# A hybrid four-mixer transformer block: element-wise steps change engine, and weight splits come in pieces

## The chip, the core and the metric

The kernel runs on one core of a Trainium2 chip. That core has TensorE (PE in the profile; its weight loads stand apart as PEld), VectorE (DVE), ScalarE (ACT), GpSimd (POOL), SyncE (SP, which issues most of the DMAs) and 16 DMA engines. The metric is the device time of one execution, in microseconds; lower is better.

## The reference, cut to what matters

One layer over 2048 tokens of width 1024. A projection feeds four mixers of width 256 each; a second projection and a SwiGLU feed-forward of width 2816 follow, with RMS norms around both.

```python
a = rms_norm(h, ln_mix_pre)
(s5_u, hg_q, hg_f, ..., fox_q, fox_k, fox_v, fox_f, ml_q, ml_k, ml_v, ...) = split(a @ w_in)
y_a = s5_mixer(...)      # complex recurrence, 16 groups
y_b = hgrn2_mixer(...)   # gated linear attention: scores(t,s) = sum_k q k exp(b_t - b_s), b = cumsum(log f)
y_c = fox_mixer(...)     # softmax(q k^T / 8 + F_t - F_s) v over all earlier tokens, head-wise RMS norm, gain
y_d = mlstm_mixer(...)   # chunked linear attention with exponential gates
h = h + rms_norm(concat[y_a, y_b, y_c, y_d] @ w_out, ln_mix_post)
a = rms_norm(h, ln_ffn_pre)
h = h + rms_norm((silu(a @ w_gate) * (a @ w_up)) @ w_down, ln_ffn_post)
```

All of it is float32. The kernel reaches that on TensorE by splitting each operand into a rounded part `hi` (type fp32r) and a rest `lo`, and adding the products hi·hi, hi·lo and lo·hi.

## The kernel before, in words

The sequence is cut into four blocks of 512 tokens. The input projection runs in two halves of two blocks each. After its first half come the mixers of block 0, in its second half the hgrn mixer of block 1 and the output projection of block 0. Then, for b = 0 to 3: output projection of b (`attn.proj`), mixers of b+1 (`mlstm_mix`, `fox_mix`, `hgrn_mix` of b+2, once `s5_mix`), feed-forward of b (`ffn`). The mixers of b+1 are written ahead of the feed-forward of b, and the two are interleaved on the engines: the program is built with `schedule_with_timeline_sim=True`, so a planner that simulates the program with its own costs sets each engine's instruction order. Every engine then runs its own queue strictly in order, and waits on semaphores.

The steps that matter here:

- `split_load` (lines 71 to 95) brings a weight tile `wr` (or `dr`) of up to 1056 columns from HBM, rounds it on ScalarE to `wh` (`dh`, line 87), and GpSimd forms the rest `wl` (`dl`, line 88) as one instruction over the whole width. Both parts are then stored for the later blocks. So weights are split only in the first pass; later passes load the stored parts.
- `fox_mix`, inner function `attend`: for each head and each tile of 128 keys, TensorE forms scores (lines 886 to 889), ScalarE takes the exponential twice, once as float32 (`f_pe`, 894) and once rounded (`f_ph`, 895), VectorE forms the rest `f_pl` (896), GpSimd adds `f_pe` to the running softmax denominators `f_accs` (900; for the first key tile it copies, 898), and TensorE multiplies with the values (903). `f_pe` lies in a ring of two buffers. The key tiles on the diagonal are narrower than 512 columns.
- `fox_mix`, inner function `output`: the normed head is multiplied with its gain on GpSimd (864).
- `hgrn_mix`: for each of two head pairs and each of the six spans h = 64 to 2 of a recursive halving, GpSimd forms the difference `hd` of the cumulative log gate and its value at the span's middle (500), ScalarE exponentiates it (504, 505), VectorE multiplies it into `hK` (507) and `hQ` (511), TensorE forms scores (521), and VectorE writes them under a mask into `hA` (525). One more difference per pair is on line 529. So a block has 14 such differences.
- `mlstm_mix`: the queries of two heads are copied into the two halves of a zero-padded tile `mQ` on GpSimd (690), four instructions in a block.

GpSimd also computes the reciprocal roots of all norms (lines 67 and 68) and sets small tiles to constants, among them the row `m01` and the tile `R` of `mlstm_mix` (lines 647, 648, 657).

Of the kernel before, what the change touches and what calls it, by code (L numbers as in the profile page):

```python
# [8 lines left out]
F32 = mybir.dt.float32  # L9
# [3 lines left out]
AF = mybir.ActivationFunctionType  # L13
ALU = mybir.AluOpType
# [4 lines left out]
P = 128  # L19
# [13 lines left out]
def f32(ap):  # L33
    return ap.bitcast(F32)
# [36 lines left out]
def split_load(c, pool, raw, tag, width, shape, src, key=None, part=None):  # L71

    nc = c.nc
    n = shape[0] * shape[1]
    hi = pool.tile([P, width], F32R, name=tag + "h", tag=tag + "h")[:, 0:n]
    lo = pool.tile([P, width], F32R, name=tag + "l", tag=tag + "l")[:, 0:n]
    if key in c.parts:  # L80
        a = part or 0
        for t, d in zip((hi, lo), c.parts[key]):
            nc.sync.dma_start(f32(t), d[:, a:a + n])
    else:
        r = raw.tile([P, width], F32, name=tag + "r", tag=tag + "r")[:, 0:n]
        nc.sync.dma_start(r.rearrange("p (k n) -> p k n", k=shape[0]), src)
        nc.scalar.activation(hi, r, AF.Copy)  # L87
        nc.gpsimd.tensor_tensor(lo, r, f32(hi), ALU.subtract)  # L88
        if key is not None:
            c.parts[key] = kept = [c.dram.tile([P, n], F32, name=f"{key}{x}") for x in "hl"]  # L90
            for t, d in zip((hi, lo), kept):
                nc.sync.dma_start(d, f32(t))
    return [x.rearrange("p (k n) -> p k n", k=shape[0]) for x in (hi, lo)]
# [76 lines left out]
def l3(t):  # L170
    return t.rearrange("p (c l) -> p c l", l=P)
# [277 lines left out]
def hgrn_mix(c, b):  # L449
    nc, tc = c.nc, c.tc  # L450
    with ExitStack() as ctx:
# [3 lines left out]
        p1, p2, ptmp = tp("h_p1", 1), tp("h_p2", 2), tp("h_tmp", 4)  # L455
# [32 lines left out]
        for p in range(2):  # L488
            A4 = hA[p].rearrange("p h (c l) -> p h c l", l=P)
            for i, h in enumerate(LEVELS):  # L490
                w = 2 * h
                nb = BLK // w
                q3 = qs[p].rearrange("p (n w) -> p n w", w=w)
                k3 = ks[p].rearrange("p (n w) -> p n w", w=w)
                Q = hQ[(7 * p + i) % nk]
                if h > 1:
                    b3 = bs[p].rearrange("p (n w) -> p n w", w=w)
                    dd = tmp("hd")
                    d3 = dd.rearrange("p (n w) -> p n w", w=w)
                    nc.gpsimd.tensor_tensor(d3, b3, b3[:, :, h - 1:h].to_broadcast([P, nb, w]), ALU.subtract)  # L500
                    ee = tmp("he")
                    eq = ee[:, 0:256].rearrange("p (n w) -> p n w", w=h)
                    ek = ee[:, 256:512].rearrange("p (n w) -> p n w", w=h)
                    nc.scalar.activation(ek, d3[:, :, 0:h], AF.Exp, scale=-1.0)
                    nc.scalar.activation(eq, d3[:, :, h - 1:2 * h - 1], AF.Exp)
                    K = hK[(7 * p + i) % nk]
                    nc.vector.tensor_tensor(K.rearrange("p (n w) -> p n w", w=w)[:, :, 0:h],
                                            k3[:, :, 0:h], ek, ALU.mult)
                    for hh in range(2):
                        s = slice(64 * hh, 64 * hh + 64)  # L510
                        nc.vector.tensor_tensor(Q[s, hh].rearrange("p (n w) -> p n w", w=h),  # L511
                                                q3[s, :, h - 1:2 * h - 1], eq[s], ALU.mult)
                else:
                    K = ks[p]
                    for hh in range(2):
                        s = slice(64 * hh, 64 * hh + 64)
                        nc.gpsimd.tensor_copy(Q[s, hh].rearrange("p (n w) -> p n w", w=1), q3[s, :, 0:1])
                pt = ps()
                p3 = pt.rearrange("p (h t) -> p h t", h=2)
                for t in range(4):  # L520
                    nc.tensor.matmul(p3[:, :, t * 64:(t + 1) * 64], lhsT=K[:, t * P:(t + 1) * P],  # L521
                                     rhs=Q[:, :, t * 64:(t + 1) * 64], start=True, stop=True)
                av = hA[p].rearrange("p h (n w) -> p h n w", w=w)[:, :, :, h - 1:2 * h - 1]
                mv = c.lvl[:, i].rearrange("p (n w) -> p n w", w=h)[:, None].to_broadcast([P, 2, nb, h])
                nc.vector.copy_predicated(av, mv, pt.rearrange("p (h n w) -> p h n w", h=2, w=h))  # L525
            q, k, bb = qs[p], ks[p], bs[p]
            b3 = l3(bb)
            e1, e2 = tmp("he1"), tmp("he2")
            nc.gpsimd.tensor_tensor(l3(e2), b3, b3[:, :, P - 1:P].to_broadcast([P, 4, P]), ALU.subtract)
            nc.scalar.activation(e1, bb, AF.Exp)  # L530
            nc.scalar.activation(e2, e2, AF.Exp, scale=-1.0)
            nc.vector.tensor_tensor(q, e1, q, ALU.mult)
            nc.vector.tensor_tensor(k, e2, k, ALU.mult)
            qes.append(q)
            kds.append(k)
            pt = ps()
            pl = pt[:, 0:8].rearrange("p (h t) -> p h t", h=2)
            for t in range(4):
                nc.tensor.matmul(pl[:, :, t], lhsT=kds[p][:, t * P:(t + 1) * P], rhs=hL[p][:, :, t],
                                 start=True, stop=True)  # L540
            nc.vector.tensor_copy(A4[:, :, :, P - 1], pl)
# [58 lines left out]
def mlstm_mix(c, b):  # L600
    nc, tc = c.nc, c.tc
    with ExitStack() as ctx:
# [82 lines left out]
        for h in range(4):  # L685
            p = h // 2
            if h % 2 == 0:
                for hh in range(2):
                    s = slice(64 * hh, 64 * hh + 64)
                    nc.gpsimd.tensor_scalar(mQ[s, hh], qs[p][s], 1.0, None, ALU.mult)  # L690
            pw_ = ps()
            nc.tensor.matmul(pw_, lhsT=c.selr[:, h], rhs=ngh, start=True, stop=False)
            nc.tensor.matmul(pw_, lhsT=c.selr[:, h], rhs=ngl, start=False, stop=False)
# [71 lines left out]
def fox_mix(c, b):  # L765
    nc, tc = c.nc, c.tc
    NK = 4 * (b + 1)
    with ExitStack() as ctx:
# [74 lines left out]
        def output(h, po, accs):  # L843
# [17 lines left out]
            nc.vector.tensor_reduce(ms, sq, AX.X, ALU.add)  # L861
            rsqrt_mean(c, ms, ms, 64)
            nc.vector.tensor_tensor(o, o, ms[:, :, None].to_broadcast([P, 4, 64]), ALU.mult)
            nc.gpsimd.tensor_tensor(o, o, gain[:, None, h * 64:h * 64 + 64].to_broadcast([P, 4, 64]), ALU.mult)
            col = 512 + h * 64
            nc.sync.dma_start(c.y_d[b][:, col:col + 64].rearrange("(t p) n -> p t n", p=P), o)

        def attend(h):
# [6 lines left out]
            for j in range(b + 1):  # L875
# [3 lines left out]
                for i in range(4):  # L879
# [8 lines left out]
                    if diag:  # L888
                        nc.tensor.matmul(pt[:, j0 * P:j0 * P + P], lhsT=c.identb, rhs=c.mask_kq,
                                         start=False, stop=True)  # L890
                    pe = p2.tile([P, 512], F32, name="f_pe", tag="pe")
                    ph = pp.tile([P, 512], F32R, name="f_ph", tag="f_p")
                    pl = pp.tile([P, 512], F32R, name="f_pl", tag="f_p")
                    nc.scalar.activation(pe[:, cs], pt[:, cs], AF.Exp)  # L894
                    nc.scalar.activation(ph[:, cs], pt[:, cs], AF.Exp)  # L895
                    nc.vector.tensor_tensor(pl[:, cs], pe[:, cs], f32(ph[:, cs]), ALU.subtract)  # L896
                    if kt == 0:
                        nc.gpsimd.tensor_copy(accs, pe)
                    else:
                        nc.gpsimd.tensor_tensor(accs[:, cs], accs[:, cs], pe[:, cs], ALU.add)  # L900
                    terms = ((V[:, i], ph, po[:, cs]), (V[:, i, 0:64], pl, po[0:64, cs]))
                    for n, (w, r, o) in enumerate(terms if kt < NK - 1 else terms[::-1]):
                        nc.tensor.matmul(o, lhsT=w, rhs=r[:, cs], start=(kt + n == 0), stop=(kt + n == NK))  # L903
# [798 lines left out]
```

## Time and profile before

| | us |
|---|---|
| median of 3 runs | 2805.01 (2796.91 to 2816.34) |
| the profiled execution's own time | 2805.62 |
| its span, first to last instruction | 2803.9 |

The profiled execution lies within 0.1% of the median, and its own time is 1.7 us more than its span. In the rows below, PE, DVE, ACT and POOL are TensorE, VectorE, ScalarE and GpSimd, and L88 is line 88 of the kernel. An instruction's duration includes the time in which it has started and is held up inside the engine.

### The profile page before, as it was taken

How to read it: one execution, taken by the hardware profiler on the slowest of the kernel's cores; microseconds unless marked ns; L12 is line 12 of the kernel's file. 1: busy time of each engine (PE TensorE's matmuls, PEld its weight loads, DVE VectorE, ACT ScalarE, POOL GpSimd, SP SyncE). 2: the span in 40 equal slices, each digit the busy share in tenths (PEclk: the TensorE clock that was granted, in tenths of full speed). 3: DMA queues.
4: the chain of work that ended last, by engine and by line, in shares of the span. 5: the costliest groups of instructions: out<-in, count | busy, mean ns of one | idle time of the engine just before them, and what ended most of it. 6: DMA issues, size and time to landing. Idle time of an engine off the chain costs nothing.

```text
span 2803.9 us, 39055 instructions
## 1 busy us (share of the span) xinstructions
PE 2692.5 (96%) x14294; PEld 2270.0 (81%) x14294; DVE 1541.4 (55%) x2522; ACT 778.3 (28%) x1502; POOL 837.9 (30%) x927
## 2 busy tenths in 40 slices
PE   6898999999999999999899999999999999999998
PEld 5787987988888778787787788888878788888886
DVE  7958466483225665865466656545666554322333
ACT  5322336233223333324221232222122331200001
POOL 7554311243125567542111234211022330100001
PEclk9899999999999999999999999999999999999999
DMA  6573696535778878696756566575656656755553
GB/s 228 195 261 123 207 293 209 169 122 210 241 230 292 287 258 282 201 310 232 255 172 214 198 195 206 177 285 187 215 181 194 202 182 230 285 195 186 193 195 135
DMA packets 323103, 605.04 MB, mean 216 GB/s; under 512 B 56160, under 2 KB 146144, under 8 KB 322656
## 3 DMA queue, kind: packets, MB, share of 16 engines
q1 hardware_dynamic: 321888, 602.48, 64.2%
q8 instruction: 113, 1.85, 0.3%
q14 instruction: 78, 0.64, 0.1%
q0 software_dynamic: 1024, 0.07, 0.0%
HBM read 428.42 MB, written 173.35 MB: 215 GB/s over the span
## 4 chain that ended last, share of the span: by engine, by line
PE 73%; DVE 9%; DMA 8%; issue 3%; POOL 2%; SPq 2%; ACT 2%; POOLq 0%; DVEq 0%; ACTq 0%
PE pf L1469 29%; PE pf L1494 15%; PE pf L1386 6%; PE pf L288 5%; PE pf L270 5%; PE ps L903 2%; DVE hQ L511 2%; PE ps L887 1%; PE ps L886 1%; PE ps L828 1%; DVE hA L525 1%; DMA b_xt<-in_x_dram 1%; PE pt L102 1%; PE ps L521 1%; DMA wh<-wu1h 1%
## 5 line engine op out<-in xcount | busy, mean ns | idle before, releaser
L1469 PE MATMUL pf<-b_ah,wh 128*128 128x512 f32 (+1 forms) x1536 | 580.5, 378 | 4.4 <-ACT b_ah L104 4.4
L1469 PE MATMUL pf<-b_ah,wl 128*128 128x512 f32 (+1 forms) x1536 | 579.8, 378 | 0.0
L1469 PE MATMUL pf<-b_al,wh 128*128 128x512 f32 (+1 forms) x1536 | 578.2, 378 | 0.0
L1494 PE MATMUL pf<-dh,g_h 128*128 128x512 f32 x1408 | 461.3, 396 | 1.8 <-DVE b_acc L1499 1.5
L1469 PEld LDWEIGHTS pf<-b_ah,wh 128*128 128x128 f32 x1536 | 291.3, 190 | 60.4 <-ACT b_ah L104 5.3
L1469 PEld LDWEIGHTS pf<-b_ah,wl 128*128 128x128 f32 x1536 | 291.3, 190 | 55.0
L1469 PEld LDWEIGHTS pf<-b_al,wh 128*128 128x128 f32 x1536 | 289.5, 189 | 54.4
L1494 PEld LDWEIGHTS pf<-dh,g_h 128*128 128x128 f32 x1408 | 264.8, 189 | 58.7 <-DVE b_acc L1499 3.4
L1494 PE MATMUL pf<-dl,g_h 128*128 128x512 f32 x704 | 277.5, 394 | 0.0
L1499 DVE TENSOR_TENSOR b_acc<-b_acc,pf 128x512 f32<-128x512 f32 x320 | 215.7, 684 | 105.9 <-PE pf L1494 103.5
L900 POOL TENSOR_TENSOR f_accs<-f_accs,f_pe 128x512 f32<-128x512 f32 (+3 forms) x144 | 172.7, 1199 | 293.6 <-ACT f_pe L894 290.7
L88 POOL TENSOR_TENSOR wl<-wr,wh 128x1024 fp32r<-128x1024 f32 (+2 forms) x76 | 185.6, 2444 | 208.6 <-ACT wh L87 137.3
L896 DVE TENSOR_TENSOR f_pl<-f_pe,f_ph 128x512 fp32r<-128x512 f32 (+3 forms) x160 | 184.6, 1162 | 88.9 <-ACT f_ph L895 75.7
L288 PE MATMUL pf<-wl,aTh 128*128 128x256 f32 (+2 forms) x768 | 220.7, 287 | 0.2 <-DMA wl<-wi_1l 0.2
L288 PE MATMUL pf<-wh,aTh 128*128 128x256 f32 (+2 forms) x768 | 220.7, 288 | 0.0
L288 PE MATMUL pf<-wh,aTl 128*128 128x256 f32 (+2 forms) x768 | 220.2, 287 | 0.0
L1473 ACT ACTIVATE g_th<-pf 128x512 f32<-128x512 f32 x88 | 52.5, 597 | 412.2 <-PE pf L1469 412.1
L1474 DVE SCALAR_TENSOR_TENSOR g_th<-g_th,pf 128x512 f32<-128x512 f32 x88 | 60.3, 685 | 191.8 <-ACT g_th L1473 191.5
L270 PE MATMUL pf<-aTh,wh 128*128 128x512 f32 (+1 forms) x400 | 158.9, 398 | 2.7 <-ACT aTh L104 2.7
L270 PE MATMUL pf<-aTh,wl 128*128 128x512 f32 (+1 forms) x400 | 157.7, 395 | 0.0
L270 PE MATMUL pf<-aTl,wh 128*128 128x512 f32 (+1 forms) x400 | 156.9, 394 | 0.1
L1475 DVE TENSOR_TENSOR g_th<-g_th,pf 128x512 f32<-128x512 f32 x88 | 60.2, 684 | 174.8 <-PE pf L1469 174.7
(510 smaller groups left out, 4812.7 us busy)
## 6 DMA issues: line engine op xcount, KB each, us to landing
dh<-wd_0h SPq DMA_DIRECT2D x66, 256.0 KB
dl<-wd_0l SPq DMA_DIRECT2D x66, 256.0 KB
dh<-wd_1h SPq DMA_DIRECT2D x66, 256.0 KB
dl<-wd_1l SPq DMA_DIRECT2D x66, 256.0 KB
wr<-in_w_ffn_gate_dram SPq DMA_DIRECT2D x22, 512.0 KB
wr<-in_w_ffn_up_dram SPq DMA_DIRECT2D x22, 512.0 KB
dr<-in_w_ffn_down_dram SPq DMA_DIRECT2D x44, 256.0 KB
f_KB<-kb_d SPq DMA_DIRECT2D x80, 132.0 KB
```

What stands on the lines that cost most here:

```text
L88: nc.gpsimd.tensor_tensor(lo, r, f32(hi), ALU.subtract)
L270: nc.tensor.matmul(l3(pt)[:, cut], lhsT=x[k][:, s], rhs=a[:, cut, k], start=(n == 0), stop=(n == 23))
L288: nc.tensor.matmul(pt[:, :w], lhsT=a[:, t, k], rhs=x[k], start=(n == 0), stop=(n == 23))
L511: nc.vector.tensor_tensor(Q[s, hh].rearrange("p (n w) -> p n w", w=h), q3[s, :, h - 1:2 * h - 1], eq[s], ALU.mult)
L896: nc.vector.tensor_tensor(pl[:, cs], pe[:, cs], f32(ph[:, cs]), ALU.subtract)
L900: nc.gpsimd.tensor_tensor(accs[:, cs], accs[:, cs], pe[:, cs], ALU.add)
L1386: nc.tensor.matmul(pt, lhsT=a[:, t, k], rhs=w, start=(first and i == 0), stop=(last and i == 2))
L1469: nc.tensor.matmul(l3(pt)[:, s], lhsT=x[:, k], rhs=a[:, s, k], start=(k == 0 and i == 0), stop=(k == KD - 1 and i == 2))
L1474: nc.vector.scalar_tensor_tensor(th, th, 1.0, pts[0], ALU.add, ALU.mult)
L1475: nc.vector.tensor_tensor(th, th, pts[1], ALU.mult)
L1494: nc.tensor.matmul(pt, lhsT=a[:, s], rhs=w[:, 0], start=(m == 0), stop=(m == 3 * len(fs) - 1))
L1499: nc.vector.tensor_tensor(acc[:, t, ns], acc[:, t, ns], pt, ALU.add)
```

## The change

Six edits. The weight rests are formed in pieces of 512 columns (1024 columns become two instructions; 1040 and 1056 three). The differences of `hgrn_mix` (lines 500 and 529), the gain of `fox_mix` (864) and the adding of the denominators (900) move from GpSimd to VectorE. The copies into `mQ` (690) move to ScalarE. The copy of the first key tile (898) is gone: for that tile the first exponential is written straight into `accs`.

```diff
-        nc.gpsimd.tensor_tensor(lo, r, f32(hi), ALU.subtract)
+        for j in range(0, n, 512):
+            s = slice(j, min(j + 512, n))
+            nc.gpsimd.tensor_tensor(lo[:, s], r[:, s], f32(hi[:, s]), ALU.subtract)
...
-                    nc.gpsimd.tensor_tensor(d3, b3, b3[:, :, h - 1:h].to_broadcast([P, nb, w]), ALU.subtract)
+                    nc.vector.tensor_tensor(d3, b3, b3[:, :, h - 1:h].to_broadcast([P, nb, w]), ALU.subtract)
...
-            nc.gpsimd.tensor_tensor(l3(e2), b3, b3[:, :, P - 1:P].to_broadcast([P, 4, P]), ALU.subtract)
+            nc.vector.tensor_tensor(l3(e2), b3, b3[:, :, P - 1:P].to_broadcast([P, 4, P]), ALU.subtract)
...
-                    nc.gpsimd.tensor_scalar(mQ[s, hh], qs[p][s], 1.0, None, ALU.mult)
+                    nc.scalar.activation(mQ[s, hh], qs[p][s], AF.Copy)
...
-            nc.gpsimd.tensor_tensor(o, o, gain[:, None, h * 64:h * 64 + 64].to_broadcast([P, 4, 64]), ALU.mult)
+            nc.vector.tensor_tensor(o, o, gain[:, None, h * 64:h * 64 + 64].to_broadcast([P, 4, 64]), ALU.mult)
...
-                    pe = p2.tile([P, 512], F32, name="f_pe", tag="pe")
+                    pe = p2.tile([P, 512], F32, name="f_pe", tag="pe") if kt else accs
...
-                    if kt == 0:
-                        nc.gpsimd.tensor_copy(accs, pe)
-                    else:
-                        nc.gpsimd.tensor_tensor(accs[:, cs], accs[:, cs], pe[:, cs], ALU.add)
+                    if kt:
+                        nc.vector.tensor_tensor(accs[:, cs], accs[:, cs], pe[:, cs], ALU.add)
```

## Rows read from the trace of the kernel before

**Rows 1.** The page, busy us of an engine, share of the span, instructions.
```profile
PE 2692.5 (96%) x14294; PEld 2270.0 (81%) x14294; DVE 1541.4 (55%) x2522; ACT 778.3 (28%) x1502; POOL 837.9 (30%) x927
```

**Rows 2.** The page, 40 equal slices: PE busy in tenths, granted clock in tenths.
```profile
PE   6898999999999999999899999999999999999998
...
PEclk9899999999999999999999999999999999999999
```

**Rows 3.** Busy us by stretch: PE, PEld, DVE, ACT, POOL; granted clock; DMA.
```profile
70.10:140.20 70.10, 56.97 (x362) 52.45 (x361) 66.01 (x184) 24.43 (x42) 41.78 (x60) 0.88 0.54 195
196.00:245.00 49.00, 37.88 (x196) 31.69 (x196) 46.07 (x65) 16.07 (x34) 28.36 (x42) 0.93 0.48 161
828.40:845.50 17.10, 15.62 (x59) 12.63 (x60) 3.17 (x7) 8.66 (x19) 13.50 (x11) 0.50 1.02 328
944.50:947.90 3.40, 3.40 (x9) 2.64 (x8) 2.71 (x5) 1.60 (x3) 1.28 (x1) 0.50 1.00 358
1111.00:1170.00 59.00, 52.48 (x267) 44.53 (x266) 50.70 (x68) 21.03 (x44) 41.59 (x44) 0.91 0.68 237
```

**Rows 4.** TensorE's waits: us in total, times, longest.
```profile
PE pt L102 <- DVE xt L239: 21.6, 5, 13.6
PE ps L521 <- DVE hQ L511: 10.6, 7, 4.1
PE ps L1118 <- DVE s_4a L1115: 9.9, 3, 4.5
...
PE ps L670 <- ACT R L666: 4.8, 1, 4.8
...
PE ps L903 <- DVE f_pl L896: 3.7, 1, 3.7
```

**Rows 5.** VectorE's groups by line and form: busy us, mean ns, idle before.
```profile
L896 DVE TENSOR_TENSOR f_pl<-f_pe,f_ph 128x512 fp32r<-128x512 f32 x112 | 151.5, 1361 | 65.9 <-ACT f_ph L895 62.8 <-issue 1.5 <-DMA wh<-wg9h 0.9
...
L533 DVE TENSOR_TENSOR hk<-he,hk 128x512 f32<-128x512 f32 x8 | 5.7, 712 | 0.0
```

**Rows 6.** GpSimd's groups by line and form.
```profile
L88 POOL TENSOR_TENSOR wl<-wr,wh 128x1024 fp32r<-128x1024 f32 x72 | 174.9, 2430 | 201.6 <-ACT wh L87 130.3 <-DMA ka_d<-flo 53.8 <-DMA dr<-in_w_ffn_down_dram 8.0
L900 POOL TENSOR_TENSOR f_accs<-f_accs,f_pe 128x512 f32<-128x512 f32 x96 | 134.3, 1399 | 213.4 <-ACT f_pe L894 211.7
L88 POOL TENSOR_TENSOR dl<-dr,dh 128x512 fp32r<-128x512 f32 x44 | 59.0, 1352 | 63.1 <-ACT dh L87 60.5 <-DMA f_QA<-qa_d 2.5
L500 POOL TENSOR_TENSOR hd<-hb 128x512 f32<-128x512 f32 x48 | 54.4, 1141 | 56.3 <-DVE hq L532 16.4 <-DMA hb<-hb_d 15.1 <-ACT he L505 9.8
```

**Rows 7.** Timeline at 938 us, fox of block 1: start, duration, engine, line.
```profile
938.34 2.42 POOL L88 TENSOR_TENSOR wl<-wr,wh 128x1024 fp32r<-128x1024 f32 x1
938.43 5.72 DVE L896 TENSOR_TENSOR f_pl<-f_pe,f_ph 128x512 fp32r<-128x512 f32 x1 [1.23 <-ACT f_ph L895]
...
940.70 0.61 POOL L898 COPY f_accs<-f_pe 128x512 f32<-128x512 f32 x1
...
941.28 2.33 POOL L88 TENSOR_TENSOR wl<-wr,wh 128x1024 fp32r<-128x1024 f32 x1
```

**Rows 8.** Timeline of GpSimd at 818 us, mlstm of block 1.
```profile
818.35 4.03 POOL L690 TENSOR_SCALAR mQ<-mq 64x512 f32<-64x512 f32 x2 [4.23 <-DMA mq<-mq_d]
822.44 0.51 POOL L647 MEMSET m<- 4x512 f32 x1
```

**Rows 9.** Timeline of VectorE at 818 us.
```profile
823.14 1.21 DVE L652 TENSOR_TENSOR_SCAN mbr<-m,mlfr 4x512 f32<-4x512 f32 x1 [2.99 <-POOL m L648]
```

**Rows 10.** Timeline at 122 us, tables of s5.
```profile
122.25 2.98 POOL L88 TENSOR_TENSOR wl<-wr,wh 128x1056 fp32r<-128x1056 f32 x1
...
122.83 2.96 DVE L1113 TENSOR_TENSOR s_O<-s_cr,s_tgp 128x512 f32<-128x512 f32 x1
```

**Rows 11.** VectorE's groups from 1111 to 1170 us, hgrn of block 2.
```profile
L511 DVE TENSOR_TENSOR hQ<-hq,he 64x256 f32<-64x256 f32 x24 | 18.8, 782 | 0.2
```

**Rows 12.** VectorE's groups from 240 to 260 us, hgrn of block 0.
```profile
L511 DVE TENSOR_TENSOR hQ<-hq,he 64x256 f32<-64x256 f32 x5 | 2.1, 417 | 0.0
```

## Prediction

> **What bounds the kernel now.** I read the page's busy shares first. TensorE is busy 96% of the span, VectorE 55%, ScalarE 28%, GpSimd 30% [rows 1]. So whatever the change does to the three others counts only where TensorE waits. All of TensorE's idle time is 2803.9 - 2692.5 = 111 us, and that is the most that any change off TensorE could win, apart from the clock. The slices show where the idle time lies: TensorE is short of full in the first two slices, and dips in a few others; from there on it is full, the feed-forward with its interleaved mixers included [rows 2]. The fox mixer of the later blocks, where most of the moved work sits, thus runs behind a full TensorE.
>
> The third view is the busy time by stretch. Three stretches have idle TensorE and a nearly full VectorE: the s5 tables (70 to 140 us: TensorE 57.0, VectorE 66.0 of 70.1), hgrn of block 0 (196 to 245 us: 37.9 and 46.1 of 49.0) and hgrn of block 2 (1111 to 1170 us: 52.5 and 50.7 of 59.0) [rows 3]. The same view shows the clock: a wait of a few microseconds is followed by a stretch at half the granted clock, such as 944.5 to 947.9 us (0.50), which then costs time again [rows 3]. The fourth view is TensorE's waits by what ended them. Of the moved steps and their neighbours, `hQ` of hgrn holds it 10.6 us in seven waits, `R` of mlstm 4.8 us in one, `f_pl` of fox 3.7 us in one [rows 4]. Small numbers against 2805: the question is which of them the change removes.
>
> **Denominators on VectorE.** 144 additions leave GpSimd, 1.40 us each at 512 columns [rows 6]. On VectorE the nearest row is the product of two 512-column tiles in SBUF, 0.712 us [rows 5]. 96 full ones cost 96 x 0.712 = 68.4 us; the 48 narrower ones have 256 columns on average, and at the 0.417 us of a 256-column product [rows 12] cost 20 us. The 16 gains add 16 x 0.417 = 6.7 us. Against that stands `f_pl`: 112 instructions of the same shape as the 0.712 us one took 1.361 us on average [rows 5], because a VectorE instruction with two inputs in SBUF stands still while GpSimd runs one of its own. One case shows it plainly: `f_pl` starts 0.09 us after a GpSimd weight rest and ends 5.72 us later, after that rest, a copy and a second rest are through [rows 7]. With the additions gone up to 112 x (1.361 - 0.712) = 72.7 us of standstill go. VectorE's balance in fox is +95 - 73 = +22 us at worst-case credit, in stretches where TensorE is full [rows 2]. The cover is TensorE's own feed-forward work; if VectorE became late there, the whole 22 us could show. I take 0 for it, and one gain: in the new kernel the copy (898) is gone and each rest is in pieces, so `f_pl` at 938 us waits for at most one piece of 1.35 us [rows 6] and ends some 5.72 - 0.71 - 1.35 = 3.7 us earlier. That is TensorE's whole wait of 3.7 us on line 903 [rows 4]. The 3.4 us at half clock behind it [rows 3] cost another 1.7 us. Together -5.4 us; the bounds are 0 (another wait takes its place) and -5.4.
>
> **Queries on ScalarE.** At 818 us the two copies into `mQ` hold GpSimd 4.03 us, with the small memset `m01` queued behind them [rows 8]; VectorE idles 2.99 us for that memset [rows 9], and what it computes then goes through `R` to the transposes of line 670, for which TensorE waits 4.8 us [rows 4]. With the copies on ScalarE the memset comes at once, and that wait shrinks by 3.0 us. The clock is at half from 828.4 to 845.5 us [rows 3]; if that came from this wait, up to 8.5 us more would be won, but no row shows that the one caused the other, so I count none of it. Sum -3.0, bounds 0 and -11.5. What it costs ScalarE isn't shown: between 0 and GpSimd's own 2.0 us each [rows 8], 16 times, so at most 32 us on an engine that is 72% idle [rows 1]. The moved copy waits for its load (4.23 us of idling [rows 8]), and on ScalarE the exponentials and tanh of the feed-forward would queue behind it. I take 0, nearest to ScalarE's idle share; 4 us a block if the planner puts it early.
>
> **Differences on VectorE.** Each block gets 14 x 0.712 = 10.0 us more on VectorE, which is the fuller engine there. In return the blocking by the 14 GpSimd differences (1.141 us each [rows 6], 16 of the 41.6 us that GpSimd is busy in block 2's stretch [rows 3]) ends. There `hQ` takes 0.782 us where it takes 0.417 us unhindered [rows 11, 12]: 24 x 0.365 = 8.8 us of standstill, and 4.4 us more if the 12 `hK` of that size are held alike, 13 us in all. If only GpSimd's share by the differences (38%) goes, 5 us are won and VectorE gets 5 us longer; if all goes, it gets 3 us shorter. The chain of a level also shortens, 1.14 to 0.71 us for its first step. I take 0, with bounds of -10 and +20 us over the two blocks in which TensorE idles; for the other two the slices are full [rows 2].
>
> **Weight rests in pieces.** 76 rests of 2.43 us become pairs of 1.35 us [rows 6]: 76 x 0.27 = 21 us more on GpSimd, hidden by its 70% of idle time. For a single VectorE instruction that arrives at random, the wait behind a piece is half as long. Where VectorE has one such instruction after another, nothing is won: a product of the shape that takes 0.7 us took 2.96 us behind a rest of 2.98 us [rows 10], and with two pieces the next product would wait behind the second. The s5 tables are such a stretch, so I take 0 for the start, with -4 to +3 us as bounds (the wait of 9.9 us on line 1118 [rows 4] is the only one there that hangs on these rests).
>
> On this the Trainium skill, page "SBUF — State Buffer", section "SBUF: two separate sides", states that VectorE and GpSimd share one port pair under an exclusive lock, held for a whole instruction, and that the loser fully blocks. By it alone, pieces halve every wait, and the start would win those 4 us. The trace doesn't agree fully: `f_pl` was held over three GpSimd instructions, not one [rows 7].
>
> **The sum** against the profiled execution's own time: 2805.6 - 5.4 - 3.0 = 2797.2 us. That execution lies 0.6 us above the median of the runs, so it is the forecast for the median as well: 2797.
>
> **The rivals.** First, nothing arrives: the planner orders the program anew with its own costs, TensorE's idle time stays at 111 us with the waits in other places, and the time is 2805. For it: the waits won are two out of dozens, and both could return as waits on the neighbouring line. Against it: both have a clear cause that the change takes away.
>
> Second, the freed VectorE reaches further (faster): half of the waits behind VectorE at the start (21.6 and 9.9 us [rows 4]) and half of the clock lost with them go. The clock costs 0.12 x 70 = 8.4 us from 70 to 140 us, 3.4 us in hgrn of block 0, 5.3 us in hgrn of block 2, and 8.5 us at 828 us [rows 3]. That gives 2797 - 15.8 - 12.8 = 2769. For it: VectorE is the late engine in each of these. Against it: in the start nothing but the pieces changes.
>
> Third, slower: in hgrn VectorE's queue gets longer without getting its standstill back, since rests and memsets on GpSimd still hold it. In the two blocks where TensorE idles that is 2 x 10.0 = 20 us, and the clock falls again behind the longer waits, another 8.7 us [rows 3]; the wins above don't come, as the additions stand ahead of `f_pl` in the same queue. That gives 2834. It decides where the standstill in a block falls by less than the 10.0 us added. For it: VectorE is busy 46.1 of 49.0 us in block 0. Against it: it was busy largely with waiting for GpSimd.
>
> **How the numbers follow.** The forecast (2790 to 2802) gets 0.5, the first rival 0.25, the second 0.15, the third 0.1. The predicted time is 2797. The range takes in the second rival at 2769 and most of the way to the third, 2769 to 2826. A change of 1%, 28 us, is about what a measurement of this kernel can tell from none: the second rival passes it in most of its cases, and the forecast's tail adds a little: faster 0.15. The third passes it in over half: slower 0.07. The rest, 0.78, lies within 1%.
>
> **What would show it.** In the changed profile `f_pl` at 512 columns falls to about 0.75 us, and no wait of TensorE on line 903 over 1 us stands. VectorE's idle time before line 652 in block 1 is gone, and the wait on `R` is under 2 us. VectorE's busy time stays within 40 us of 1541, GpSimd's falls by at least 134 + 54 - 21 = 167 us [rows 6]. TensorE's idle time falls from 111 to about 103 us. In hgrn of blocks 0 and 2 the stretch has the same length within 5 us; if it is 10 us longer, the third rival holds. The prediction is wrong if the planner's new order opens waits that rows of before don't show, such as a mixer that ends after the feed-forward it is hidden behind.

## The result, and the profile after

The changed kernel takes 2780.93 us (median of 5 runs, 2779.70 to 2783.66), the kernel before 2808.53 us on the same chip (5 runs, 2796.91 to 2816.34): a ratio of 0.9915, with a 95% interval of 0.9894 to 0.9937. So it is 0.85% faster, inside the range and 16 us below the forecast of 2797. The profiled executions differ by 24.7 us of span (2803.9 to 2779.2 us).

The page of the changed kernel, busy us, then TensorE and its granted clock in 40 slices:

```profile
PE 2679.5 (96%) x14294; PEld 2259.5 (81%) x14294; DVE 1543.4 (56%) x2738; ACT 788.5 (28%) x1518; POOL 587.5 (21%) x759
...
PE   6899999999999999899899999999999999999998
...
PEclk9999999999999999999999999999999999999999
```

Against [rows 1, 2], GpSimd lost 250 us and VectorE gained 2, although it got 216 more instructions. TensorE's idle time fell from 111.4 to 2779.2 - 2679.5 = 99.7 us, and its records at half clock (the last microseconds left out) from 78.3 to 57.8 us; half of 20.5 is 10.3 us. These two make 22.0 of the 24.7 us. TensorE's waits in the changed kernel (lines from 88 to 896 stand two further down than before, those from 903 on are the same; in u1_nofox, e1_gain and e3_adds below all of them stand two further down, and in p1_fox line 903 is 901):

```profile
PE pt L104 <- DVE xt L241: 18.7, 5, 13.8
PE pf L290 <- ACT stg L316: 8.4, 1, 8.4
PE ps L523 <- DVE hQ L513: 7.0, 4, 4.7
...
PE pf L1386 <- ACT junk L1332: 5.6, 1, 5.6
...
PE ps L1118 <- DVE s_4a L1115: 2.5, 2, 1.7
...
PE ps L672 <- ACT R L668: 1.7, 1, 1.7
```

Beside [rows 4]: the wait on `f_pl` is gone, that on `R` fell from 4.8 to 1.7 us, that on `s_4a` from 9.9 to 2.5 us, and a new one of 8.4 us stands on line 290, at 97 us. VectorE's groups by form (busy us, mean ns, idle before):

```profile
L898 DVE TENSOR_TENSOR f_pl<-f_pe,f_ph 128x512 fp32r<-128x512 f32 x96 | 71.4, 743 | 8.9 <-PE ps L903 4.5 <-ACT f_ph L897 3.3 <-PE ps L891 1.1
...
L900 DVE TENSOR_TENSOR f_accs<-f_accs,f_pe 128x512 f32<-128x512 f32 x96 | 70.5, 734 | 30.3 <-ACT f_pe L896 30.0
...
L502 DVE TENSOR_TENSOR hd<-hb 128x512 f32<-128x512 f32 x48 | 34.2, 718 | 13.3 <-DMA hb<-hb_d 11.0 <-ACT he L507 2.0
```

`f_pl` fell from 1361 ns [rows 5] to 743, and the moved additions take 734 ns, the differences 718 ns, where GpSimd took 1399 and 1141 [rows 6].

**Where the time came from.** All these kernels run the same 14294 matmuls. So I add up the matmuls' columns in the order in which TensorE runs them, and read at equal sums how far one trace is ahead of the other. Counting each matmul as at least 256 columns gives the values here and in the table below within 0.3 us; counting the columns as they are moves single values by up to 1.6 us and changes no reading. Against before the changed kernel is 0.3 us ahead at 568 us (time of before), 8.6 at 617, 8.2 at 821, 13.6 at 854, 15.5 at 936, 21.1 at 961, and 24.3 near the end. Three short stretches of before thus hold 19 of 24.7 us: the hgrn mixer of block 1 (568 to 617 us), the mlstm mixer of block 1 (821 to 854) and one place in its fox mixer (936 to 961). The start won some microseconds and had given them back by 485 us.

### The profile page after: what moved, and what is told of

It reads as the page before. It is cut to its first block, busy times and chain, and to the rows that moved or that the text cites. A ratio compares the mean times of both kernels' runs of the same rounds, so it can differ in the third digit from the quotient of the medians.

```text
span 2779.2 us, 38978 instructions
## 1 busy us (share of the span) xinstructions
PE 2679.5 (96%) x14294; PEld 2259.5 (81%) x14294; DVE 1543.4 (56%) x2738; ACT 788.5 (28%) x1518; POOL 587.5 (21%) x759
## 3 DMA queue, kind: packets, MB, share of 16 engines
q0 software_dynamic: 1024, 0.07, 0.0%
## 4 chain that ended last, share of the span: by engine, by line
PE 79%; DVE 8%; DMA 7%; POOL 2%; issue 2%; ACT 2%; SPq 1%; POOLq 0%; DVEq 0%; ACTq 0%
PE pf L1469 32%; PE pf L1494 16%; PE pf L290 6%; PE pf L1386 6%; PE pf L272 5%; PE ps L903 2%; PE ps L889 1%; PE ps L888 1%; PE ps L830 1%; DMA wr<-in_w_in_dram 1%; DMA b_xt<-in_x_dram 1%; DVE hA L527 1%; PE ps L523 1%; DVE hQ L513 1%; PE pt L104 1%
## 5 line engine op out<-in xcount | busy, mean ns | idle before, releaser
L90 POOL TENSOR_TENSOR wl<-wr,wh 128x512 fp32r<-128x512 f32 (+2 forms) x156 | 213.2, 1389 | 247.2 <-ACT wh L87 183.5
L1494 PEld LDWEIGHTS pf<-dl,g_h 128*128 128x128 f32 x704 | 132.9, 189 | 26.9
L290 PEld LDWEIGHTS pf<-wh,aTh 128*128 128x128 f32 x768 | 145.8, 190 | 11.0 <-ACT stg L316 8.6
```

Source lines behind the costliest of these rows:

```text
L90: nc.gpsimd.tensor_tensor(lo[:, s], r[:, s], f32(hi[:, s]), ALU.subtract)
L290: nc.tensor.matmul(pt[:, :w], lhsT=a[:, t, k], rhs=x[k], start=(n == 0), stop=(n == 23))
L1494: nc.tensor.matmul(pt, lhsT=a[:, s], rhs=w[:, 0], start=(m == 0), stop=(m == 3 * len(fs) - 1))
```

## The experiments

Theory A, from the prediction: each edit takes away its own wait, and the effects add. Theory B, the first rival's mechanism: the planner orders the whole program anew after any edit, and gains and losses fall on places that the edit doesn't touch. All kernels compute the whole reference. Four runs make one part alone in the kernel before.

```diff
p1_fox (the denominators alone)
-            nc.gpsimd.tensor_tensor(o, o, gain[:, None, h * 64:h * 64 + 64].to_broadcast([P, 4, 64]), ALU.mult)
+            nc.vector.tensor_tensor(o, o, gain[:, None, h * 64:h * 64 + 64].to_broadcast([P, 4, 64]), ALU.mult)
...
-                    pe = p2.tile([P, 512], F32, name="f_pe", tag="pe")
+                    pe = p2.tile([P, 512], F32, name="f_pe", tag="pe") if kt else accs
...
-                    if kt == 0:
-                        nc.gpsimd.tensor_copy(accs, pe)
-                    else:
-                        nc.gpsimd.tensor_tensor(accs[:, cs], accs[:, cs], pe[:, cs], ALU.add)
+                    if kt:
+                        nc.vector.tensor_tensor(accs[:, cs], accs[:, cs], pe[:, cs], ALU.add)
p2_mq (the queries alone)
-                    nc.gpsimd.tensor_scalar(mQ[s, hh], qs[p][s], 1.0, None, ALU.mult)
+                    nc.scalar.activation(mQ[s, hh], qs[p][s], AF.Copy)
p3_diff (the hgrn differences alone; line 529 likewise)
-                    nc.gpsimd.tensor_tensor(d3, b3, b3[:, :, h - 1:h].to_broadcast([P, nb, w]), ALU.subtract)
+                    nc.vector.tensor_tensor(d3, b3, b3[:, :, h - 1:h].to_broadcast([P, nb, w]), ALU.subtract)
p4_pieces (the pieces alone)
-        nc.gpsimd.tensor_tensor(lo, r, f32(hi), ALU.subtract)
+        for j in range(0, n, 512):
+            s = slice(j, min(j + 512, n))
+            nc.gpsimd.tensor_tensor(lo[:, s], r[:, s], f32(hi[:, s]), ALU.subtract)
```

p1_fox: 

> Only the denominators, the gain and the copy of the first key tile are changed. Theory (each edit takes away its own wait): TensorE's wait of 3.7 us on line 903 in the fox mixer of block 1 is gone, and the half-clock stretch behind it; 5 to 8 us shorter, about 2802. The waits on R (4.8 us) and on hQ (10.6 us) stay. Rival (the planner's new order makes the gain): the time moves by more than 8 us either way, or the wait on line 903 stays. Rival (the pieces made the gain in fox): f_pl is still held behind a whole weight rest of 2.4 us, TensorE still waits over 1 us on line 903.

p2_mq: 

> Only the copies into mQ move to ScalarE. Theory: the wait on R in mlstm of block 1 falls from 4.8 to under 2 us and the half-clock stretch there gets shorter; 3 to 6 us shorter, about 2804. All other waits of TensorE stay as before. Rival (planner): waits at other places change by as much or more.

p3_diff: 

> Only the hgrn differences move to VectorE. Theory: the stretch of hgrn of block 1 (556 to 617 us of before), where the changed kernel is about 8 us shorter, is shorter here by 6 to 9 us; the total about 2800. Rival (it takes all edits together, since VectorE's standstill behind whole weight rests stays): hgrn gets no shorter, or longer by up to 10 us a block, total 2805 to 2830.

p4_pieces: 

> Only the weight rests come in pieces of 512 columns. Theory (pieces spread the standstill but do not lessen it where VectorE is full): the total stays within 5 us of before, 2804 to 2813; the first 140 us are no shorter than 2 us. Rival (the pieces make the gain at the start and in fox): 8 to 15 us shorter, with the waits on lines 903 and 1118 gone.

The next four are the kernel before once more, unchanged, and the changed kernel with one part undone, by the same lines the other way round: u1_nofox without the denominators' part, u3_nodiff without the differences, u4_nopieces without the pieces.

b_again: 

> The kernel before, unchanged, profiled once more. It shows how much of a place's wait belongs to the program and how much to the one execution. Theory (waits belong to the instruction order): TensorE's waits on line 903 (3.7 us) and on R (4.8 us), and the half-clock stretches behind them, are there again within 1 us each. Rival (they are chance of one execution, such as when a weight load lands): either is gone or half as long. Total 2795 to 2812 either way.

u1_nofox: 

> The changed kernel with the denominators, the gain and the copy of the first key tile left on GpSimd as before. Theory (edits add up, and this one alone cost 6 us): 4 to 8 us faster than the changed kernel, about 2770 to 2777 where before is 2802. Rival (it gains beside the others, since it frees GpSimd for the pieces): slower than the changed kernel by 5 us or more.

u3_nodiff: 

> The changed kernel with the hgrn differences back on GpSimd. Theory (edits add up; the differences alone gained 14 us): about 12 to 16 us slower than the changed kernel, 2788 to 2793, with the stretch of hgrn of block 1 longer by about 7 us. Rival (the edits all take away the same waits in block 1, so any of them will do): within 4 us of the changed kernel.

u4_nopieces: 

> The changed kernel with weight rests in one piece. Theory (edits add up; the pieces alone gained 11 us): 8 to 13 us slower than the changed kernel, 2784 to 2790. Rival (any of the edits takes away the same waits): within 4 us of the changed kernel.

The last four take the denominators' part to pieces. e1_gain, e2_copy and e3_adds each put one of its three steps into u1_nofox. e4_two leaves the queries and the differences alone: u1_nofox without the pieces.

```diff
e1_gain (against u1_nofox)
-            nc.gpsimd.tensor_tensor(o, o, gain[:, None, h * 64:h * 64 + 64].to_broadcast([P, 4, 64]), ALU.mult)
+            nc.vector.tensor_tensor(o, o, gain[:, None, h * 64:h * 64 + 64].to_broadcast([P, 4, 64]), ALU.mult)
e2_copy (against u1_nofox)
-                    pe = p2.tile([P, 512], F32, name="f_pe", tag="pe")
+                    pe = p2.tile([P, 512], F32, name="f_pe", tag="pe") if kt else accs
...
-                    if kt == 0:
-                        nc.gpsimd.tensor_copy(accs, pe)
-                    else:
+                    if kt:
                         nc.gpsimd.tensor_tensor(accs[:, cs], accs[:, cs], pe[:, cs], ALU.add)
e3_adds (against u1_nofox)
-                        nc.gpsimd.tensor_tensor(accs[:, cs], accs[:, cs], pe[:, cs], ALU.add)
+                        nc.vector.tensor_tensor(accs[:, cs], accs[:, cs], pe[:, cs], ALU.add)
e4_two (against u1_nofox)
-        for j in range(0, n, 512):
-            s = slice(j, min(j + 512, n))
-            nc.gpsimd.tensor_tensor(lo[:, s], r[:, s], f32(hi[:, s]), ALU.subtract)
+        nc.gpsimd.tensor_tensor(lo, r, f32(hi), ALU.subtract)
```

e1_gain: 

> The changed kernel without the denominators, in which the fox edit is left out, plus the 16 gains on VectorE alone. Theory (the fox edit costs through the planner's new order, not through its own work): an edit as small as this also moves the time by more than 4 us either way, through waits that have nothing to do with the gain, such as the one of the output projection of block 1 on ScalarE's square sums. Rival (it costs through VectorE's added work of 100 us): no more than 2 us from the kernel without the fox edit, 2764 to 2768.

e2_copy: 

> The kernel without the fox edit, plus only this: the first exponential of the first key tile is written into the denominators, so that GpSimd's 16 copies are gone; the additions stay on GpSimd. Theory (planner's order): more than 4 us either way, in waits elsewhere. Rival (work): 0 to 2 us faster, since only work is removed, 2763 to 2766.

e3_adds: 

> The kernel without the fox edit, plus only the 144 additions on VectorE; the first copy and the gain stay on GpSimd. Rival (work): it carries the whole cost of the fox edit, 2778 to 2783, and the time is lost in the fox stretches, where VectorE has become fuller. Theory (planner's order): the time may be anywhere from 2763 to 2783, and what is lost is lost outside the fox stretches, at the output projection of block 1 and in mlstm of block 1.

e4_two: 

> Only the queries on ScalarE and the hgrn differences on VectorE, weight rests in one piece, fox as before. Theory (the pieces are worth nothing of their own; what they won alone came from the order): within 4 us of the kernel without the fox edit, 2762 to 2770. Rival (the pieces shorten VectorE's standstill, 11 us as when done alone): 2774 to 2780.

**All results.** Median and ratio to the kernel before on the same chip, then from the one profiled execution of each: the span less 2803.9 us, and what was won (-) or lost (+) in four stretches of before, at equal sums of columns as above: hgrn of block 1, mlstm of block 1, fox of block 1, and the second output projection (1344 to 1394 us).

| kernel | median us | ratio (95%) | span | hgrn(1) | mlstm(1) | fox(1) | proj(1) |
|---|---|---|---|---|---|---|---|
| b_again | 2807.08 | 1.0004 (0.9989 to 1.0019) | -1.4 | -1.0 | -2.1 | +0.4 | -0.9 |
| p1_fox | 2808.05 | 1.0022 (1.0008 to 1.0035) | +2.7 | +2.0 | -5.4 | -0.6 | +1.3 |
| p2_mq | 2797.09 | 0.9978 (0.9963 to 0.9994) | -16.4 | -3.7 | -8.4 | -5.6 | +0.3 |
| p3_diff | 2788.65 | 0.9946 (0.9926 to 0.9967) | -14.8 | -6.9 | -4.1 | -5.5 | -0.8 |
| p4_pieces | 2791.83 | 0.9957 (0.9942 to 0.9971) | -12.1 | -0.9 | -3.3 | -5.5 | +1.0 |
| u3_nodiff | 2790.16 | 0.9956 (0.9940 to 0.9973) | -10.5 | -2.4 | -9.4 | -5.1 | +0.9 |
| u4_nopieces | 2779.10 | 0.9913 (0.9893 to 0.9933) | -27.8 | -8.2 | -10.0 | -5.6 | -0.2 |
| the changed kernel | 2780.93 | 0.9915 (0.9894 to 0.9937) | -24.7 | -8.3 | -5.4 | -5.6 | +0.2 |
| e3_adds | 2782.21 | 0.9925 (0.9903 to 0.9948) | -24.7 | -8.5 | -10.5 | -5.3 | 0.0 |
| e1_gain | 2775.68 | 0.9897 (0.9870 to 0.9924) | -24.9 | -7.6 | -3.6 | -5.6 | -9.4 |
| e4_two | 2777.25 | 0.9909 (0.9887 to 0.9931) | -28.5 | -7.5 | -10.0 | -5.7 | -9.6 |
| e2_copy | 2770.23 | 0.9882 (0.9861 to 0.9904) | -39.9 | -7.6 | -10.3 | -5.0 | -9.3 |
| u1_nofox | 2765.63 | 0.9867 (0.9844 to 0.9890) | -42.0 | -7.6 | -10.1 | -5.5 | -9.4 |

Each kernel has one profiled execution. That of p2_mq took 7.8 us less than the kernel's median, and that of e1_gain 5.1 us more, so their spans don't stand for their medians. The runs come from several chips, so kernels are compared by their ratios.

The effects don't add. With queries and differences always in, a table of four ratios is complete: neither other part 0.9909 (e4_two), pieces alone 0.9867, denominators alone 0.9913 (u4_nopieces), both 0.9915. The pieces win 0.42% where the denominators stay on GpSimd and nothing where they don't; the denominators lose 0.48% beside the pieces and nothing without them. The intervals of u1_nofox and e4_two just touch.

**The order.** The traces show whether the planner's order is the same. In b_again every instruction of TensorE, VectorE, ScalarE and GpSimd stands at the same place of its queue as in the kernel before. In each of the twelve changed kernels only 8404 to 11134 of TensorE's 14294 matmuls do. So theory B's premise holds: any of the edits gives a new order of the whole program. Which gain or loss comes from the order has to be read place by place.

**What the expectations were worth.** In p2_mq and p3_diff the named place gained what theory A says. But both also won 5.5 us in fox, which no wait of theirs explains, and p3_diff's whole gain is 15 us where some 5 were expected. u3_nodiff lost about what was expected of it. In b_again the waits are there again, the one on `R` 1.2 us shorter where 1 us was allowed. p1_fox, p4_pieces, u1_nofox and u4_nopieces missed theory A's times; p4_pieces hit the 8 to 15 us of its rival, but not at the start. e4_two missed its theory's 2762 to 2770 and hit its rival's 2774 to 2780; whether the rival's reason holds is taken up under the pieces. e1_gain and e2_copy lie within the noise of u1_nofox and decide nothing. e3_adds carries the whole price of the denominators' part.

**hgrn of block 1** is where theory A holds best. The stretch from 560 to 615 us, busy us of PE, PEld, DVE, ACT and POOL, granted clock; first before, then p3_diff (which runs 6 us later here), then the changed kernel:

```profile
560.00:615.00 55.00, 48.93 (x316) 43.74 (x315) 47.60 (x81) 17.71 (x43) 28.03 (x42) 0.97 0.33 112
```

```profile
560.00:615.00 55.00, 53.61 (x363) 49.11 (x362) 44.65 (x94) 16.50 (x42) 13.38 (x29) 1.00 0.45 159
```

```profile
560.00:615.00 55.00, 55.00 (x352) 48.96 (x351) 51.78 (x99) 18.24 (x44) 8.08 (x22) 1.00 0.46 158
```

VectorE's groups in the same stretch, before and in p3_diff, and between them GpSimd's differences before:

```profile
L511 DVE TENSOR_TENSOR hQ<-hq,he 64x256 f32<-64x256 f32 x24 | 15.2, 632 | 0.5 <-POOL hQ L469 0.2
```

```profile
L500 POOL TENSOR_TENSOR hd<-hb 128x512 f32<-128x512 f32 x12 | 13.8, 1161 | 13.1 <-DMA hb<-hb_d 4.8 <-DVE hq L532 3.6 <-ACT he L505 1.8
```

```profile
L511 DVE TENSOR_TENSOR hQ<-hq,he 64x256 f32<-64x256 f32 x24 | 10.2, 425 | 0.2
L500 DVE TENSOR_TENSOR hd<-hb 128x512 f32<-128x512 f32 x12 | 8.3, 696 | 4.5 <-DMA hb<-hb_d 4.3
```

TensorE was idle for 6.1 us of these 55 before (waits of 0.63, 0.68, 1.17 and 3.60 us), and the clock was at half for 3.4 us. With the differences on VectorE `hQ` falls from 632 to 425 ns, and a difference takes 0.70 us where GpSimd took 1.16. All of VectorE's instructions of this mixer sum up to 48.8 us in p3_diff where they took 44.0 (88 against 74): it does more work, and TensorE waits less. That each span's chain begins sooner is the likely reason; no run separates it from the rest. In every kernel with the differences the stretch is 6.9 to 8.5 us shorter, without half clock; without them it moves by -3.7 to +2.0, with 3.4 to 6.8 us of it. Chance has a share here too: the 3.60 us are a copy queued behind three convolution steps on VectorE, and the same wait is 1.96 us in b_again, whose order is the same, 4.23 us in p1_fox and 1.5 to 2.0 us in p2_mq, p4_pieces and u3_nodiff. In all, TensorE's waits of over 0.3 us in this mixer sum up to 2.7 to 6.1 us in the six traces without the differences' part, and to at most 1.4 us in the eight with it.

**mlstm of block 1.** The wait on `R` is 0.4 to 2.0 us in all nine kernels with the queries on ScalarE and 3.2 to 4.8 us in the five traces without. The clock stands behind it, but not in step. In those five it is at half for 6.8 to 17.1 us (17.1 after the wait of 4.8 us, 13.7 after 3.6 in b_again). In the nine it is at half for 10.2 us after 1.7 (the changed kernel), for 13.7 after 2.0 (e1_gain), for 3.4 after 0.4 (p2_mq), and not at all there in the other six, whose waits are 0.4 to 1.2 us. The same 10.3 us in the changed kernel and in u1_nofox:

```profile
821.10:831.40 10.30, 10.30 (x41) 8.26 (x39) 2.08 (x3) 7.24 (x18) 8.37 (x9) 0.50 0.89 282
```

```profile
821.10:831.40 10.30, 10.17 (x76) 8.77 (x75) 2.08 (x3) 8.38 (x20) 8.26 (x9) 1.00 0.77 259
```

41 matmuls against 76, in a TensorE that is busy in both. This is the 5 us by which the changed kernel won less here than u1_nofox. It is not the planner's doing: from 700 to 860 us these two, e1_gain, e2_copy, e3_adds and u3_nodiff run the same order on all four engines, and two of the six have the half clock. What tips it isn't shown.

**fox of block 1** speaks against theory A. In the kernel before, run again, the two waits of the prediction repeat:

```profile
PE ps L903 <- DVE f_pl L896: 4.0, 1, 4.0
PE ps L670 <- ACT R L666: 3.6, 1, 3.6
```

Of the other kernels only the one that moves the denominators alone waits on `f_pl` for more than 0.3 us, whether the denominators moved or not (in e4_two neither they nor the rests are touched). The longest `f_pl` takes 5.72 us before, 5.71 in b_again and 5.18 in p1_fox, and at most 2.79 us in the eleven others, four of which have whole rests. The timeline of p1_fox:

```profile
936.92 4.70 POOL L88 TENSOR_TENSOR wl<-wr,wh 128x1024 fp32r<-128x1024 f32 x2
937.01 5.18 DVE L896 TENSOR_TENSOR f_pl<-f_accs,f_ph 128x512 fp32r<-128x512 f32 x1 [1.23 <-ACT f_ph L895]
...
942.24 0.45 PE L901 MATMUL ps<-f_pl,f_V 128*64 128x512 f32 x1 [3.13 <-DVE f_pl L896]
```

The copy and the additions are gone from GpSimd, and `f_pl` is still held over two whole rests, 5.18 us instead of 5.72 [rows 7]. What ends this wait is where the planner puts two rests next to one `f_pl`; any edit but this one parted them.

**The second output projection** shows theory B at its plainest. Between 1270 and 1345 us neither VectorE nor GpSimd runs an instruction of fox in u1_nofox, e1_gain, e3_adds or the changed kernel, and of the edited lines only the weights' rests and the copies into `mQ` stand there, edited alike in all four. Yet u1_nofox wins 9.4 us here, and with the additions on VectorE (e3_adds) nothing is won. Busy us by engine from 1288 to 1345 us, first in the changed kernel, then in u1_nofox:

```profile
1288.00:1345.00 57.00, 48.56 (x202) 38.93 (x201) 23.63 (x30) 14.17 (x29) 7.09 (x13) 0.91 0.90 309
```

```profile
1288.00:1345.00 57.00, 56.91 (x259) 46.15 (x259) 31.56 (x39) 16.60 (x36) 11.67 (x19) 1.00 0.86 325
```

The changed kernel waits here 2.8 us for the gated activations and 5.6 us for the squares (`junk`), and the clock is at half for 3.4 and 6.8 us. e3_adds, with nothing but the additions put into u1_nofox, has both waits again:

```profile
PE pf L1388 <- ACT junk L1334: 5.5, 1, 5.5
...
PE pf L1496 <- ACT g_h L1480: 2.9, 1, 2.9
```

The squares themselves take 0.6 us each. They wait for VectorE's step `b_acc<-pf`, which reads the same results of the projection, and that step is queued behind the last two steps of the feed-forward of block 0, which wait for the load of `g_h` (the tile `g_h1` of the code). VectorE, then ScalarE in the changed kernel:

```profile
1326.91 1.28 DVE L1531 SCALAR_TENSOR_TENSOR g_h<-b_acc,g_rs,g_h 128x1024 f32<-128x1024 f32 x1 [6.92 <-DMA g_h<-h_d]
1330.66 1.28 DVE L1531 SCALAR_TENSOR_TENSOR g_h<-b_acc,g_rs,g_h 128x1024 f32<-128x1024 f32 x1 [2.46 <-DMA g_h<-h_d]
1332.05 2.48 DVE L1395 TENSOR_TENSOR b_acc<-pf,g_h 128x512 f32<-128x512 f32 x4
1333.11 0.60 ACT L1332 ACTIVATE junk<-pf 128x512 bf16<-128x512 f32 x1 [14.38 <-DVE b_acc L1395]
```

and VectorE in u1_nofox:

```profile
1317.81 2.58 DVE L1533 SCALAR_TENSOR_TENSOR g_h<-b_acc,g_rs,g_h 128x1024 f32<-128x1024 f32 x2 [10.86 <-DMA g_h<-h_d]
1320.49 2.48 DVE L1397 TENSOR_TENSOR b_acc<-pf,g_h 128x512 f32<-128x512 f32 x4
```

The projection begins at 1305.0 us in the changed kernel and at 1299.9 us in u1_nofox. So the last of these steps starts 25.6 us after that in the one and some 19 us in the other. This parts all traces: in the ten that wait on `junk` here for 5.4 to 7.4 us it starts 25.3 to 27.7 us after the projection's first matmul, in the four that don't (u1_nofox, e1_gain, e2_copy, e4_two) 17.9 to 19.2 us. These loads take turns in two buffers with `b_y`, which TensorE transposes. Its order, in the changed kernel:

```profile
1305.02 0.39 PE L1386 MATMUL pf<-wh,b_ah 128*128 128x512 f32 x1
...
1306.62 1.03 PE L104 MATMUL pt<-ident,b_y 128*128 128x128 f32 x8
```

and in u1_nofox:

```profile
1292.26 1.03 PE L104 MATMUL pt<-ident,b_y 128*128 128x128 f32 x8
...
1299.89 0.39 PE L1388 MATMUL pf<-wh,b_ah 128*128 128x512 f32 x1
```

The planner puts the last eight transposes 1.6 to 2.6 us behind the projection's first matmul in the ten traces, and 7.6 to 7.7 us ahead of it in the four. That this order makes the loads late is read from the times and the shared buffers; no run changes it by itself.

So the price of the denominators' part is not paid in fox: there the additions did what was said of them. VectorE's `f_pl`, in u1_nofox and in e3_adds:

```profile
L898 DVE TENSOR_TENSOR f_pl<-f_pe,f_ph 128x512 fp32r<-128x512 f32 x112 | 142.2, 1275 | 85.2 <-ACT f_ph L897 74.0 <-PE ps L905 5.9 <-DMA wu6l<-wl 2.9
```

```profile
L898 DVE TENSOR_TENSOR f_pl<-f_pe,f_ph 128x512 fp32r<-128x512 f32 x112 | 85.9, 767 | 27.4 <-ACT f_ph L897 24.0 <-PE ps L905 3.3
```

The 16 gains alone (e1_gain) stand 0.30% above u1_nofox, but the intervals overlap, so nothing is shown. The profile of e1_gain loses 4.6 us against that of u1_nofox by 485 us and 6.5 us in mlstm(1). Up to 510 us all four engines run the same order in both, and TensorE does up to 983 us. So this is how far two executions of one order can lie apart. e2_copy has u1_nofox's TensorE order from first to last; its 0.15% are within the noise too.

**The pieces** win 0.42% between e4_two and u1_nofox. The profiles differ by 13.5 us, of which 4.8 us lie in the feed-forward of block 0 (854 to 936 us). VectorE and TensorE in e4_two, then VectorE in u1_nofox:

```profile
865.71 2.42 DVE L794 CAST f_KB<-f_ot 4x512 fp32r<-4x512 f32 x3
868.16 1.27 DVE L807 TENSOR_TENSOR_SCAN f_fk<-one,fcar,ps 4x512 f32<-4x512 f32 x1
869.36 1.25 DVE L1497 COPY b_acc<-pf 128x512 f32<-128x512 f32 x2
870.06 0.50 PE L1494 MATMUL pf<-dh,g_h 128*128 128x512 f32 x1 [2.67 <-DVE b_acc L1497]
```

```profile
867.42 0.65 DVE L1499 COPY b_acc<-pf 128x512 f32<-128x512 f32 x1
868.11 3.28 DVE L796 CAST f_KB<-f_ot 4x512 fp32r<-4x512 f32 x3
```

TensorE waits 2.67 us in e4_two, with 3.4 us at half clock behind it, for a copy that is queued behind three casts and a scan; in u1_nofox the copy stands ahead of the casts. p2_mq and u4_nopieces have e4_two's order and the same wait of 2.69 us. The three casts take no longer beside whole rests (2.42 us) than beside pieces (3.28 us). Another 5.9 us lie after 1394 us, where no weight is split any more. So at least 10.7 of the 13.5 us are not shorter holds behind rests, which is what e4_two's rival took them for.

**The best version** is u1_nofox: pieces, queries and differences, with the denominators left on GpSimd. At 0.9867 it beats both kernels, the changed one by 0.48%, some 13 us; e2_copy and e1_gain, which add a step each, can't be told from it.

## Why the prediction was right, and where not

**Total.** The forecast sum was -8.4 us, the profile gave -24.7. The sign and the range hold. But 2781 lies outside the band of 2790 to 2802 that got half of the chance, and nearer to the second rival's 2769 (12 us) than to the forecast (16 us); it is the width of the range that took it in. The largest term of the sum had a wrong reason, and the largest gain stood in it at 0.

**Denominators (-5.4).** The size met what happened, by luck: fox(1) won 5.6 us, the wait of 3.7 us is gone and so are the 3.4 us at half clock. The step that failed is "in the new kernel the copy (898) is gone and each rest is in pieces, so `f_pl` at 938 us waits for at most one piece". e4_two loses the wait with copy and whole rests in place, and p1_fox keeps it (3.1 us) without the copy. I took a meeting of one instruction with three others, decided by the planner's order, for a property of the code. Alone this part gains nothing (1.0022). The wait's half clock came and went with it.

**VectorE's balance in fox (0, at worst +22).** Right: VectorE's busy time rose by 2 us in all, and `f_pl` fell to 743 ns for the 0.75 said. On this the Trainium skill, page "SBUF — State Buffer", section "SBUF: two separate sides", has VectorE and GpSimd share a port pair under a lock held for a whole instruction. The fall from 1275 to 767 ns with the additions alone agrees. That pieces halve every wait, as the prediction drew from the rule, doesn't show. With the additions still on GpSimd `f_pl` averages 1275 ns with pieces (u1_nofox) and 1279 without (e4_two).

**Queries (-3.0, bounds 0 and -11.5).** The mechanism is right and the term was too small. The wait on `R` fell by 3.1 us as said, VectorE's idle time ahead of `mbr` from 2.99 us [rows 9] to 0.0, and a copy takes 0.63 us on ScalarE where two took 4.03 us on GpSimd [rows 8]. The half clock that I left out belongs to it in part: 17.1 us fell to 10.2 here, and to none in six other kernels, though with the same order it comes and goes. mlstm(1) gave 5.4 us, in the kernels without that rest of half clock 9.4 to 10.5. Alone this part gives 0.22%, some 6 us.

**Differences (0).** The step that failed is "for the other two the slices are full [rows 2]". A slice is 70 us long; in the hgrn mixer of block 1 it hid 6.1 us of idle TensorE in 55. My estimate for VectorE (5 us of standstill won, VectorE 5 us longer) fits what p3_diff shows there, 44.0 to 48.8 us; that a longer VectorE can still let TensorE wait less I named (the chain's first step) and didn't price. In block 0, where I looked for it, all eight kernels with the differences win 2.6 to 8.6 us from 196 to 245 us, while the others lose 0.9 to 4.9, but p3_diff and the changed kernel have given that back by 300 us. In block 2 (1111 to 1170 us) their lead changes by under 4 us. Alone this part gives 0.54%, the most of all four.

**Pieces (0, bounds -4 and +3 at the start).** At the start it came out so: the wait on `s_4a` fell by 7.4 us, a new one of 8.4 us on line 290 came with it, and by 485 us all kernels with pieces but u3_nodiff are within 4 us of before. Alone the pieces give 0.43%, of which 5.5 us lie in fox(1) and 3.3 in mlstm(1), where p3_diff gained as much without pieces; removed from the changed kernel they cost nothing (0.9913). That is order and not shorter holds, as far as the places above show it.

**The rivals.** The first, that the planner's order moves the waits elsewhere, was half of the truth: the order governs proj(1) and fox(1), but it also wins, where the rival had it put the waits elsewhere. The second's 2769 came nearer to the time than the forecast, but its places were wrong: the start gave nothing. The third is refuted: no hgrn mixer got 10 us longer. From 196 to 300 us the lead of the kernels with the differences changes by -4.5 to +2.0 us, and from 1111 to 1200 us by -1.4 to +5.7 us, where b_again shows +2.6 and +3.8 (+ is lost).

**Still open.** There is one profile for each kernel. In the table's four stretches b_again, with the same order, shows up to 2.1 us without any change, but e1_gain and u1_nofox, alike there too, lie 6.5 us apart in mlstm(1). So only what repeats is safe: hgrn(1) (eight kernels with the differences against six traces without), fox(1) (eleven against three) and proj(1) (four against ten). Which of the planner's own costs moves the transposes in proj(1) wasn't tried. A kernel with the queries left on GpSimd and the other parts in place wasn't run.

## What to carry to other kernels

Where a planner orders the whole program, a single wait in one profile is no term of a sum: run the unchanged code under two harmless edits, and count a wait only if it stays. A gain that the code itself carries (here an engine's standstill that ends in a stretch with idle TensorE) stays in every order; look for it with windows as short as the stage, not with the page's slices. Before a difference between two traces is explained, compare the order of their instructions: here 4.6 and 6.5 us lay between two traces of the same order. And try each part of a combined change both alone and left out: here three parts beat all four by some 13 us.

## What was not expected of the hardware

Behind waits of nearly the same length on `R`, 1.2 and 1.7 us, and with the same order of instructions, TensorE's granted clock stayed at full in one kernel and fell to half for 10.2 us in the other; half of that is more than the wait itself. And one VectorE instruction stood still over two GpSimd instructions in a row (5.18 us over 4.70 us of rests) and once over three (5.72 us [rows 7]), so it doesn't always get in between two of them.
